# Norms of A's q and of C's q rank applied ahead of the scores, and softmax sums divided out of A's and C's outputs instead of their probabilities

## The chip, the cores and the metric

The kernel runs on one core of a Trainium2 chip. The metric is the device time of one execution in microseconds (us), as the median of several runs.

A core has five engines that run side by side and wait for each other through semaphores. PE (TensorE) multiplies matrices: it loads a stationary operand of up to 128x128 (shown as PEld) and streams the moving one past it, into a bank of PSUM. DVE (VectorE) does elementwise work and reductions, ACT (ScalarE) functions and copies, POOL (GpSimd) elementwise work at a lower rate, and SP (SyncE) issues the transfers (DMA) between memory and SBUF, the working memory. Each engine takes its own instructions in the order in which they were written to its queue.

## The reference

A bidirectional encoder of two layers on 512 tokens and 1024 channels, in float32. Each layer:

```python
h = rms_norm(x, ln1_g)
a_q, a_k, a_v, b_q, b_k, b_v, c_cq, c_ckv, c_kr, gates = split(h @ w_in)
# A: 8 heads of 64, 2 kv heads; q and k normed per head, then 2-D rotary
q = axial(rms_norm(a_q, q_g)) * 64 ** -0.5;  k = axial(rms_norm(a_k, k_g))
y_a = softmax(q k^T) v
# B: 8 heads with two maps of 32 each
p = softmax(q0 k0^T) - lam * softmax(q1 k1^T);  y_b = rms_norm(p v, sub_g) * (1 - lambda_init)
# C: latent attention; ranks 384 and 256, 8 heads of 64 + 32 rotary
q = rms_norm(c_cq, g) @ w_uq;  kv = rms_norm(c_ckv, g) @ w_ukv
y_c = softmax((q_nope k_nope^T + q_rope k_rope^T) * 96 ** -0.5) v
x = x + sum_n(sigmoid(gate_n) * (y_n @ w_branch_n)) @ w_out
x = x + relu(rms_norm(x, ln2_g) @ w_ff1) ** 2 @ w_ff2
```

and a last norm at the end.

## The kernel before

**Precision.** Products run in float32r, with each float32 operand split into a high part and a low rest. `hi` (ACT, L150) writes the high part, `lo` (DVE, L155, or L157 with a scale) the rest, `split` does both. A weight is fetched by SP, its high part `wh` is made by ACT (L60) and its rest `wl` by POOL or DVE (L63); in the attention stages all of these are POOL's. Each product is the sum of high x high, high x low and low x high, three matmuls.

**Order of the work.** `plan` lists items with a cost in us of products; `run` emits them in that order, fetching and splitting weights some us ahead. `defer(dt, f)` emits `f` once `dt` us of products have been emitted after the present point; `want` emits what is still due until a needed tile exists. `weave` spreads one list of items (gates, projections) between the items of another (attention). From the emitted program the order on each engine is then planned once, with estimated durations, before it runs; so an engine may have later work ahead of earlier work, but on the chip its order is fixed.

**Stages of a layer.** Projection of A's k and v, statistics of the stream, A's q (two halves of four heads, `a_q`), the start of B's q and k; A's attention, woven with the rest of B's projections; B's attention, woven with gates, A's branch products, C's ranks (`c_proj`), C's rotary (`c_rope`), values and first heads (`c_pair`); C's attention, woven with further gates and heads; the merge of the gated branches; the output product; the MLP.

**Attention.** `attend` has 32 units per mixer: a head and a tile of 128 queries. For each unit `probs` makes the scores (PE, two banks "S"), their maximum (DVE, L510) and the exponential with the sum over keys (ACT, L515). 5.5 us of products later the probabilities are turned (PE, four 128x128 transposes, L526) and split (L529 ACT, L530 DVE); 6.0 later they meet v (`pv`). After a head's four tiles `fix` adds two halves of the product (L539 ACT, L540 DVE); after a pair of heads `finish` makes the split output `y`, which the branch products read.

Where the change touches it:
- *A's q.* `post` of `a_q` makes the rotary of the raw q as two terms (`a_rope`: DVE, and half of the second term on POOL, L407) and adds them (L433). `late`, 14 us of products on, turns the rows (L263) and splits them (`a_G`), then calls `norm`: squares on POOL (L416), sums (L418), and the reciprocal roots `aR` (`rsqrt`, a dozen small DVE instructions, L169 to L180). `aR` isn't put on q: it multiplies the maximum (L514) and is the scale of the exponential.
- *C's q rank.* `rank` splits the raw rank straight out of PSUM, and late_q makes the factor `rq` from its sums of squares (L747, `rsqrt`, L755). `rq` scales the scores, as `aR` does. The kv rank is normed itself: diagonals of the factor (L302), a product that spreads it over the partitions, and a multiplication (L769).
- *Sums.* For A and C `normalise` takes the reciprocal of the sum (L519) and scales the 128x512 probabilities (L520).
- *B.* Its second map's weight is the reciprocal of its sum (L671) times minus lambda and the first map's sum (L672); L673 adds the second map's probabilities with this weight to the first's. B's output norm takes the first map's sum out again. Its `finish` spreads eight factors per pair to 128x512 (`bR`, L695), turns them on PE (`bT`, L702) and multiplies (L703).

Of the kernel before, what the change touches and what calls it, by code (L numbers as in the profile page):

```python
# [25 lines left out]
# pieces of 1024 columns per layer  # L26
# [11 lines left out]
# columns of the gain array  # L38
# [3 lines left out]
class Weight:  # L42
    """A piece of weights: loaded, then split into two float32r parts that add up to it."""
# [24 lines left out]
class Trunk:  # L68
# [24 lines left out]
    def run(self, plan):  # L93
        """Emits the items (cost, function, weights), the weights' loads and splits ahead of their use."""
# [29 lines left out]

# [41 lines left out]
    def rsqrt(self, dst, v, n):  # L166
# [5 lines left out]
        # a step of Newton's, then one of third order  # L172
# [30 lines left out]
    def tm_chunk(self, ws, per, width, xs, evac, post=None, late=None, lag=12.0, tags="LLLL"):  # L203
        """Items of a token-major product: one for each tile of 128 tokens, or, with weights in
        two pieces, one for each of these and each piece, two tiles to a bank."""
# [21 lines left out]
        def half(u, tt):  # L227
# [4 lines left out]
            for i, (l, r) in enumerate(p):  # L232
                # the bank's first product clears it for both tiles
# [25 lines left out]
    def transpose4(self, src, sl, name="tp"):  # L259
        """[tokens, 4, cols] of 128 columns to [128, 512 tokens] in a bank."""  # L260
# [6 lines left out]
    def stat_add(self, st, d, x):  # L267
        """Sums of squares over d = 0, 2, 4, 6 and over 1, 3, 5, and the squares of 7."""
# [15 lines left out]
    def col_sums(self, ps, xs, tts=range(4)):  # L284
        """Sums over the partitions of all of xs, a column for each 128 tokens, in one group."""
# [24 lines left out]
    def bcast_cols(self, col, name):  # L310
        """[128 tokens, 4] to [128, 512 tokens], the same row in each partition."""
# [31 lines left out]
    def layer_consts(self, l):  # L343
# [4 lines left out]
        # gains of A's q and k in the rotary tables  # L348
# [13 lines left out]
        # minus lambda of B  # L362
# [22 lines left out]
    def v_evac(self, vt, tt, ps, scale):  # L385
        """128 columns of two heads to [hi|lo] of the first and [lo|hi] of the second."""
# [5 lines left out]
    def a_rope(self, tq, nh, n):  # L392
        """Gain and axial rotary of each head's 64 columns, as the two terms of a sum."""
# [18 lines left out]
    def head_sumsq(self, e, x, sq, nh):  # L412
        """[128, 4 nh] sums of squares over each head's 64 columns."""
# [7 lines left out]
    def a_q(self, l, g):  # L421
        """The rows' norms of q stay out of it: they scale the scores."""
# [8 lines left out]
        def post():  # L431
            t1, t2 = self.a_rope(st["t"], 4, "q")
            nc.vector.tensor_tensor(t1, t1, t2, op=ALU.add)  # L433
            st["r"], st["f"] = t1, t2

        def norm():
            ss = self.head_sumsq(nc.gpsimd, st["t"], st["f"], 4)
# [3 lines left out]
            self.aR[g] = self.p.tile([128, 16], F32, tag="a_R", name="a_R", bufs=2)  # L441
            self.rsqrt(self.aR[g], ss, 16)

        def late():
# [8 lines left out]
            norm()  # L453
# [50 lines left out]
    def probs(self, mms, scale=None, z=None):  # L504
        """Scores of 128 queries: their exponentials and the sums of these."""
# [7 lines left out]
        if scale is not None:  # L513
            nc.vector.tensor_tensor(m, m, scale, op=ALU.mult)  # L514
        nc.scalar.activation(p, s, AF.Exp, bias=m, scale=1.0 if scale is None else scale, accum_out=z)  # L515
        return p, z

    def normalise(self, p, z):
        self.nc.vector.reciprocal(z, z)  # L519
        self.nc.vector.tensor_scalar(p, p, z, None, op0=ALU.mult)  # L520
# [21 lines left out]
    def attend(self, unit_probs, vt, finish, cost):  # L542
        """Items for the 8 heads' 4 tiles of queries; finish(pair, y) takes a pair's output."""
# [30 lines left out]
    def att_a(self):  # L574
        self.y = {}

        def probs(h, qt):
# [4 lines left out]
            i = qt * 4 + h % 4  # L582
            p, z = self.probs([(G[:, e, q], K[:, 0]), (G[r, e, q], K[r, 1])], self.aR[g][:, i : i + 1])
            self.normalise(p, z)
# [16 lines left out]
    def b_qk(self, l, n, hb):  # L601
        """q or k of four heads: rotary on the first 8 of each map's 32, then features on partitions."""
# [41 lines left out]
    def b_stack(self, h):  # L644
        """A head's two maps: q as [hi; lo; hi] and k as [hi; hi; lo] on 96 partitions."""
# [9 lines left out]
    def att_b(self, l):  # L655
        nc = self.nc

        def probs(h, qt):
            """The maps' difference times the first map's sum: the norm takes that out again."""
# [6 lines left out]
            if h % 2 == 0 and qt == 0:  # L666
                self.bz[h // 2] = self.p.tile([128, 8], F32, tag="bz", name="bz", bufs=2)
            i = 2 * qt + h % 2
            p0, z0 = self.probs([(Q[0:96, 0, q], K[0:96, 0])], z=self.bz[h // 2][:, i : i + 1])
            p1, z1 = self.probs([(Q[0:96, 1, q], K[0:96, 1])])  # L670
            nc.vector.reciprocal(z1, z1)  # L671
            nc.vector.scalar_tensor_tensor(z1, z1, self.nlam, z0, op0=ALU.mult, op1=ALU.mult)  # L672
# [12 lines left out]
        def sums(j, yt, sq):  # L685
# [4 lines left out]
            z = self.bz[j]  # L690
# [3 lines left out]
            R = self.tmp("bR", (128, 4, 2, 64))  # L694
            nc.vector.tensor_copy(R, rs.rearrange("p (t h) -> p t h", h=2).unsqueeze(3).to_broadcast([128, 4, 2, 64]))  # L695
            self.defer(3.0, lambda: scale(j, yt, R))

        def scale(j, yt, R):
            T = self.ps("T", "bT")
            Rf = R.rearrange("p t h f -> p t (h f)")  # L700
            for tt in range(4):
                nc.tensor.transpose(T[:, tt * 128 : (tt + 1) * 128], Rf[:, tt], self.ident)  # L702
            nc.vector.scalar_tensor_tensor(yt, yt, self.gsub, T, op0=ALU.mult, op1=ALU.mult)  # L703
# [7 lines left out]
    def c_proj(self, l):  # L711
        """The ranks' features on partitions; the norm of q's rank scales the scores."""
# [3 lines left out]
        def rank(n, j, gi, w):  # L716
            def f():
# [32 lines left out]
        def late_q():  # L750
            self.cf["q"] = st["q"]
            v = norm("q", 384)
            self.rq = self.p.tile([128, 4], F32, tag="c_rq", name="c_rq", bufs=1)
            self.rsqrt(self.rq, v, 4)
            nc.vector.tensor_scalar(self.rq, self.rq, C_SCALE, None, op0=ALU.mult)  # L755

        def late_kv():
            v = norm("kv", 256)
# [453 lines left out]
```

## Time and profile before

| | |
|---|---|
| median of 3 runs | 1964.0 us (1963.39 to 1965.02) |
| span of the profiled execution | 1961.6 us |
| share of the span: PE / PEld / DVE / ACT / POOL | 97% / 80% / 63% / 47% / 22% |

The profile is of one execution. Its span runs from the program's first to its last instruction; 1961.6 us of span stand against 1964.0 us of the median run. The page has parts: busy time of each engine; the chain of work that ended last; groups of instructions (source line, engine, operation, what is written and read, shapes, count, then busy time, mean duration of one, and the idle time of the engine in front of them with what ended it). Other views show the busy time by stretches of the span, the waits (engine and line that waited, for whom, us in total, times, longest), and single instructions in the order of time. Matmuls are pipelined: the time from one start to the next is what one costs PE, not its duration.

### The profile page before, as it was taken

Reading aid. Unit: us, or ns where it says so; the run is one execution under the profiler, and the core shown is the slowest. Engines: PE = TensorE matmul, PEld = TensorE weight load, DVE = VectorE, ACT = ScalarE, POOL = GpSimd, SP = SyncE. Lnnn points to the kernel's source line nnn. Section 1 sums busy time; section 2 is a strip of 40 time slices with the busy share of each in tenths; the row PEclk is TensorE's granted clock in tenths of the full one; section 3 lists DMA queues with packets and bytes.
Section 4 is the critical chain, followed back from the end, with each engine's and each line's share of the span. In section 5 each row is a group of like instructions: output and inputs, shape, how many; then the busy total and the mean of one; then the engine's idle time right before and its main releaser. Section 6 shows DMA issues by size and latency. Waiting matters only on the chain.

```text
span 1961.6 us, 26144 instructions
## 1 busy us (share of the span) xinstructions
PE 1893.2 (97%) x9848; PEld 1569.0 (80%) x9848; DVE 1227.5 (63%) x2232; ACT 916.9 (47%) x1658; POOL 427.1 (22%) x259
## 2 busy tenths in 40 slices
PE   8999989999999999999999999999999999999997
PEld 8888777777778888888898877777777788888886
DVE  7788888856665443444477889796565654334434
ACT  5466665754534331243245666556554334213332
POOL 4211232344235000000041112323431440000000
PEclk9999999999999999999999999999999999999998
DMA  4212322222123222223322033213230432223222
GB/s 156 67 41 69 109 79 68 80 80 91 45 93 122 97 97 97 97 97 113 113 92 65 28 96 103 83 44 96 79 93 33 137 99 91 97 95 102 98 96 68
DMA packets 63150, 171.83 MB, mean 88 GB/s; under 512 B 9520, under 2 KB 14000, under 8 KB 63024
## 3 DMA queue, kind: packets, MB, share of 16 engines
q1 hardware_dynamic: 63024, 170.16, 27.2%
q8 instruction: 78, 1.28, 0.3%
q14 instruction: 48, 0.39, 0.1%
HBM read 149.15 MB, written 4.19 MB: 78 GB/s over the span
## 4 chain that ended last, share of the span: by engine, by line
PE 78%; DVE 14%; ACT 3%; issue 2%; DMA 1%; SPq 1%; POOL 0%; DVEq 0%; POOLq 0%; ACTq 0%
PE ff L147 35%; PE gate L147 12%; PE sc L147 6%; PE br L147 5%; PE tm L234 5%; PE out L147 4%; PE pT L526 4%; PE pv L147 4%; PE c_rank L147 2%; DVE mg L919 1%; DVE mx L514 1%; DVE mx L510 1%; ACT p L515 1%; DVE p L673 1%; DVE wl L63 1%
## 5 line engine op out<-in xcount | busy, mean ns | idle before, releaser
L60 ACT CAST wh<-wr 128x1024 fp32r<-128x1024 f32 (+5 forms) x310 | 292.0, 942 | 645.8 <-PE ff L147 430.9
L63 POOL TENSOR_TENSOR wl<-wr,wh 128x1024 fp32r<-128x1024 f32 (+4 forms) x170 | 326.8, 1924 | 768.4 <-ACT wh L60 714.6
L63 DVE TENSOR_TENSOR wl<-wr,wh 128x1024 fp32r<-128x1024 f32 (+2 forms) x140 | 171.9, 1228 | 281.3 <-ACT wh L60 281.2
L147 PE MATMUL ff<-ff,wh 128*128 128x512 f32 (+1 forms) x1056 | 317.2, 383 | 0.0
L147 PE MATMUL ff<-xg,wh 128*128 128x512 f32 x1024 | 315.5, 389 | 0.0
L147 PE MATMUL gate<-xg,wh 128*128 128x512 f32 x768 | 243.5, 396 | 1.1 <-DVE c_K L155 1.1
L147 PEld LDWEIGHTS ff<-ff,wh 128*128 128x128 f32 x1056 | 196.3, 188 | 38.6
L147 PEld LDWEIGHTS ff<-xg,wh 128*128 128x128 f32 x1024 | 192.1, 188 | 39.6
L510 DVE TENSOR_REDUCE mx<-sc 128x1 f32<-128x512 f32 x256 | 174.0, 684 | 50.3 <-PE sc L147 49.6
L234 PE MATMUL tm<-wh,xg 128*128 128x256 f32 x1024 | 204.4, 291 | 0.0
L147 PE MATMUL ff<-ff,wl 128*128 128x512 f32 (+1 forms) x528 | 202.0, 383 | 0.0
L147 PE MATMUL ff<-xg,wl 128*128 128x512 f32 x512 | 199.4, 389 | 0.0
L147 PEld LDWEIGHTS gate<-xg,wh 128*128 128x128 f32 x768 | 141.4, 188 | 33.0 <-issue 4.4
L234 PEld LDWEIGHTS tm<-wh,xg 128*128 128x128 f32 x1024 | 165.8, 193 | 1.0 <-issue 0.5
L277 POOL TENSOR_TENSOR acc<-acc,sq 128x512 f32<-128x512 f32 x15 | 24.6, 1641 | 626.9 <-ACT sq L275 626.9
L529 ACT CAST pt<-pT 128x512 fp32r<-128x512 f32 x192 | 111.9, 584 | 84.3 <-PE pT L526 83.1
L530 DVE TENSOR_TENSOR pt<-pT,pt 128x512 fp32r<-128x512 f32 x192 | 131.4, 686 | 30.7 <-ACT pt L529 30.1
L147 PE MATMUL gate<-xg,wl 128*128 128x512 f32 x384 | 150.4, 392 | 0.0
L234 PE MATMUL tm<-wl,xg 128*128 128x256 f32 x512 | 145.8, 285 | 0.0
L526 PE MATMUL pT<-ident,p 128*128 128x128 f32 x768 | 120.5, 280 | 10.7 <-DVE p L673 8.6
L526 PEld LDWEIGHTS pT<-ident,p 128*128 128x128 f32 x768 | 87.6, 141 | 40.8 <-issue 26.2
L147 PEld LDWEIGHTS ff<-ff,wl 128*128 128x128 f32 x528 | 99.2, 188 | 19.5
(239 smaller groups left out, 3196.1 us busy)
## 6 DMA issues: line engine op xcount, KB each, us to landing
wr<-w SPq DMA_DIRECT2D x234, 512.0 KB, 3.5
wr<-w SPq DMA_DIRECT2D x52, 256.0 KB, 2.6
b_sq<-b_f SPq DMA_DIRECT2D x96, 64.0 KB, 2.4
b_sk<-b_f SPq DMA_DIRECT2D x96, 64.0 KB, 2.0
x<-xT SPq DMA_DIRECT2D x8, 256.0 KB, 5.6
c_Q<-c_qr SPq DMA_DIRECT2D x32, 64.0 KB, 2.4
c_K<-c_krf SPq DMA_DIRECT2D x16, 128.0 KB, 4.4
x<-xT SPq DMA_DIRECT2D x4, 512.0 KB, 6.0
```

The costliest lines, as they stand in the source:

```text
L60: t.nc.scalar.copy(wh, self.raw)
L63: e.tensor_tensor(wl, self.raw, wh.bitcast(F32), op=ALU.subtract)
L147: self.nc.tensor.matmul(out, l, r, start=(i == 0), stop=(i == n - 1))
L234: self.nc.tensor.matmul(ps, l, r, start=(u == 0 and i == 0 and tt % 2 == 0), stop=(u == 1 and tt % 2 == 1 and i == len(p) - 1))
L277: e.tensor_tensor(st[d % 2], st[d % 2], sq, op=ALU.add)
L510: nc.vector.tensor_reduce(m, s, axis=AX.X, op=ALU.max, negate=True)
L514: nc.vector.tensor_tensor(m, m, scale, op=ALU.mult)
L515: nc.scalar.activation(p, s, AF.Exp, bias=m, scale=1.0 if scale is None else scale, accum_out=z)
L526: nc.tensor.transpose(T[:, k], p[:, k * 128 : (k + 1) * 128], self.ident)
L529: nc.scalar.copy(h[:, :, q], T)
L530: nc.vector.tensor_tensor(lo[:, :, q], T, h[:, :, q].bitcast(F32), op=ALU.subtract)
L673: nc.vector.scalar_tensor_tensor(p0, p1, z1, p0, op0=ALU.mult, op1=ALU.add)
```

## The change

Four edits:
1. `a_q` squares the raw q on POOL at the start of `post`, ahead of the rotary. 3 us of products after `post`, `norm` makes the sums and reciprocal roots and multiplies the rotated rows, 128x1024, by them (DVE). `late` turns rows that are normed.
2. The q rank of C is treated as the kv rank: kept whole, and 9 + 2 us of products later multiplied by its spread factor and split.
3. Scores of A and C come out ready, so `probs` has no scale. Probabilities stay undivided. Each unit's sum goes to a column of a tile of eight per pair (`zcol`, three buffers, for B too); when a pair's output is there, `finish_plain` takes eight reciprocals, spreads them (`spread_pair`, B's code moved), and 2.5 us of products later turns them on PE, multiplies the output and splits it.
4. B's weight: `tensor_scalar` with two pointer scalars instead of `scalar_tensor_tensor`.

```diff
@@ a_q
         def post():
+            sq = self.s4("a_qs", (128, 4, 256), F32)
+            nc.gpsimd.tensor_tensor(sq, st["t"], st["t"], op=ALU.mult)
             t1, t2 = self.a_rope(st["t"], 4, "q")
             nc.vector.tensor_tensor(t1, t1, t2, op=ALU.add)
-            st["r"], st["f"] = t1, t2
+            st["r"], st["sq"] = t1, sq
+            self.defer(3.0, norm)
 
         def norm():
-            ss = self.head_sumsq(nc.gpsimd, st["t"], st["f"], 4)
+            ss, rs = self.small("ss", 16), self.small("a_R", 16)
+            nc.vector.tensor_reduce(ss, st["sq"].rearrange("p t (h f) -> p (t h) f", f=64), axis=AX.X, op=ALU.add)
...
-            self.aR[g] = self.p.tile([128, 16], F32, tag="a_R", name="a_R", bufs=2)
-            self.rsqrt(self.aR[g], ss, 16)
+            self.rsqrt(rs, ss, 16)
+            r = st["r"].rearrange("p t (h f) -> p (t h) f", f=64)
+            nc.vector.tensor_tensor(r, r, rs.unsqueeze(2).to_broadcast([128, 16, 64]), op=ALU.mult)
...
                 self.aG[2 * g + j] = G
-            norm()
@@ probs
-        if scale is not None:
-            nc.vector.tensor_tensor(m, m, scale, op=ALU.mult)
-        nc.scalar.activation(p, s, AF.Exp, bias=m, scale=1.0 if scale is None else scale, accum_out=z)
+        nc.scalar.activation(p, s, AF.Exp, bias=m, accum_out=z)
...
-    def normalise(self, p, z):
-        self.nc.vector.reciprocal(z, z)
-        self.nc.vector.tensor_scalar(p, p, z, None, op0=ALU.mult)
+    def zcol(self, h, qt):
+        if h % 2 == 0 and qt == 0:
+            self.zs[h // 2] = self.p.tile([128, 8], F32, tag="bz", name="bz", bufs=3)
+        i = 2 * qt + h % 2
+        return self.zs[h // 2][:, i : i + 1]
+
+    def spread_pair(self, rs):
+        R = self.tmp("bR", (128, 4, 2, 64))
+        self.nc.vector.tensor_copy(R, rs.rearrange("p (t h) -> p t h", h=2).unsqueeze(3).to_broadcast([128, 4, 2, 64]))
+
+        def turn():
+            T = self.ps("T", "bT")
+            Rf = R.rearrange("p t h f -> p t (h f)")
+            for tt in range(4):
+                self.nc.tensor.transpose(T[:, tt * 128 : (tt + 1) * 128], Rf[:, tt], self.ident)
+            return T
+
+        return turn
@@ finish_plain
         def f(j, yt):
+            rs = self.small("rz", 8)
+            self.nc.vector.reciprocal(rs, self.zs[j])
+            turn = self.spread_pair(rs)
+            self.defer(2.5, lambda: scale(j, yt, turn))
+
+        def scale(j, yt, turn):
+            self.nc.vector.tensor_tensor(yt, yt, turn(), op=ALU.mult)
             y = self.s4(f"y{n}")
             self.split(y, yt)
@@ att_b
-            nc.vector.scalar_tensor_tensor(z1, z1, self.nlam, z0, op0=ALU.mult, op1=ALU.mult)
+            nc.vector.tensor_scalar(z1, z1, self.nlam, z0, op0=ALU.mult, op1=ALU.mult)
@@ c_proj
-                if n == "q":
-                    x = self.s4("c_f")
-                    self.split(x, ps, g)
-                else:
-                    if j == 0:
-                        st["raw"] = self.s4("c_sq", dtype=F32)
-                    x = st["raw"][:, j]
-                    self.hi(x, ps, g)
+                if j % 2 == 0:
+                    st["raw"] = self.s4("c_sq", dtype=F32)
+                x = st["raw"][:, j % 2]
+                self.hi(x, ps, g)
...
         def late_q():
-            self.cf["q"] = st["q"]
-            v = norm("q", 384)
-            self.rq = self.p.tile([128, 4], F32, tag="c_rq", name="c_rq", bufs=1)
-            self.rsqrt(self.rq, v, 4)
-            nc.vector.tensor_scalar(self.rq, self.rq, C_SCALE, None, op0=ALU.mult)
+            dg = factor("q", 384, C_SCALE)
+            self.defer(2.0, lambda: spread("q", dg))
...
+        def spread(n, dg):
             ps = self.ps("T", "c_bc")
             self.spread(ps, dg)
             f = []
-            for x in st["kv"]:
+            for x in st[n]:
                 nc.vector.tensor_tensor(x, x, ps, op=ALU.mult)
                 f.append(self.s4("c_f"))
                 self.split(f[-1], x)
-            self.cf["kv"] = f
+            self.cf[n] = f
```

In A's and C's `probs` the scale argument and the call of `normalise` go.

More of the change, by code (lines that the diff above doesn't have):

```diff
@@ L574, in att_a @@
     def att_a(self):
-        self.y = {}
         def probs(h, qt):
@@ L693, in sums, with scale @@
             self.rsqrt(rs, v, 8)
[L694 to L703, printed above, removed]
+            turn = self.spread_pair(rs)
+            self.defer(3.0, lambda: scale(j, yt, turn))
+        def scale(j, yt, turn):
+            nc.vector.scalar_tensor_tensor(yt, yt, self.gsub, turn(), op0=ALU.mult, op1=ALU.mult)
             y = self.s4("yb")
@@ L750, in late_q, with factor @@
         def late_q():
[L751 to L764 removed]
+            dg = factor("q", 384, C_SCALE)
+            self.defer(2.0, lambda: spread("q", dg))
+        def late_kv():
+            dg = factor("kv", 256)
+            self.defer(2.0, lambda: spread("kv", dg))
+        def factor(n, width, scale=None):
+            r = self.small("c_r", 4)
+            self.rsqrt(r, norm(n, width), 4)
+            if scale is not None:
+                nc.vector.tensor_scalar(r, r, scale, None, op0=ALU.mult)
+            return self.diags(r)
+        def spread(n, dg):
             ps = self.ps("T", "c_bc")
@@ L935, in begin @@
         def begin():
-            self.aG, self.aK, self.aR, self.ys = {}, {}, {}, {"a": {}, "b": {}, "c": {}}
-            self.bz = {}
+            self.aG, self.aK, self.ys = {}, {}, {"a": {}, "b": {}, "c": {}}
+            self.zs = {}
             self.bf, self.bs, self.bV = {"q": {}, "k": {}}, {"q": {}, "k": {}}, {}
```

22 lines of the change are left out of this document (5 added, 17 removed).

## The prediction

> **What bounds the kernel now.** I read the page's busy times first, then busy time by stage, then what PE (TensorE) waits for, then single rows.
>
> ```profile
> span 1961.6 us, 26144 instructions
> PE 1893.2 (97%) x9848; PEld 1569.0 (80%) x9848; DVE 1227.5 (63%) x2232; ACT 916.9 (47%) x1658; POOL 427.1 (22%) x259
> ```
>
> PE is busy 97% of the span; only what is added to PE, or a wait of PE that goes or comes, can move the end. By stage of layer 0 (columns: stretch, its length, busy time and count of PE, PEld, DVE, ACT, POOL, granted clock, DMA share, GB/s):
>
> ```profile
> 55.00:71.00 16.00, 13.66 (x115) 13.45 (x113) 15.31 (x35) 6.63 (x11) 1.89 (x1) 0.99 0.25 91
> 75.00:187.00 112.00, 108.38 (x751) 91.23 (x750) 89.06 (x202) 69.81 (x146) 18.30 (x9) 0.98 0.16 48
> 187.00:369.00 182.00, 169.22 (x904) 139.66 (x903) 155.90 (x325) 113.48 (x247) 53.73 (x31) 0.98 0.29 84
> 369.00:577.00 208.00, 206.43 (x994) 160.49 (x993) 128.58 (x250) 109.04 (x203) 74.23 (x46) 1.00 0.24 75
> 577.00:590.00 13.00, 8.20 (x32) 5.65 (x31) 10.55 (x8) 3.77 (x5) 6.32 (x3) 0.86 0.56 195
> ```
>
> The rows are: end of the layer's first projections, A's attention, B's, C's, the merge behind C. In A's and C's attention PE has 3.6 and 1.6 us of idle time: the vector work taken out of these loops is work off the path. DVE (VectorE) is full at 55 to 71 (15.31 of 16) and nearly so in B. What PE waits for, both layers together:
>
> ```profile
> PE sc L147 <- ACT p L515: 10.4, 6, 2.7
> PE pT L526 <- DVE p L673: 8.6, 8, 2.1
> PE tp L263 <- DVE b_t L620: 4.7, 6, 1.5
> PE pv L147 <- DVE pt L530: 4.3, 4, 1.5
> PE tp L263 <- DVE a_G L155: 3.4, 2, 2.3
> ```
>
> The first, second and fourth, 23.3 us, are the attentions' vector chains, nearly all in B; this is what relief of DVE can win there at most.
>
> **What goes from DVE.** Groups (busy, mean ns of one):
>
> ```profile
> L514 DVE TENSOR_TENSOR mx<-mx,c_rq 128x1 f32<-128x1 f32 x64 | 30.0, 468 | 1.6
> L514 DVE TENSOR_TENSOR mx<-mx,a_R 128x1 f32<-128x1 f32 x64 | 20.5, 320 | 0.9
> L519 DVE RECIPROCAL z<-z 128x1 f32<-128x1 f32 x128 | 20.6, 161 | 24.0 <-ACT p L515 18.5
> L520 DVE TENSOR_SCALAR p<-p,z 128x512 f32<-128x512 f32 x128 | 62.8, 491 | 3.2
> L672 DVE SCALAR_TENSOR_TENSOR z<-z,nlam,bz 128x1 f32<-128x1 f32 x64 | 30.8, 481 | 1.1
> L671 DVE RECIPROCAL z<-z 128x1 f32<-128x1 f32 x64 | 10.2, 160 | 10.4 <-ACT p L515 9.6
> ```
>
> A and C lose 30.0 + 20.5 + 20.6 + 62.8 = 133.9 us of DVE time. In A's and C's loops this covers the new reciprocal, copy and product of each pair (at most L519's 0.16, and twice L520's 0.49 for a copy and a product of the same size: 1.1 a pair, 18 us for 16 pairs), so I cost those at nothing, except for the layer's last pair of C (below). If that cover were gone, A's stage (89 of 112 us busy) would still have room for the 4.6 us of its four pairs. The buffer that each pair's spread now takes costs nothing as long as A and C hold no more such tiles than B's stage does; bounded by the same rows of waits, since a late buffer would show as a wait for DVE.
>
> **What comes to PE.** Each of 16 pairs gets four transposes of the spread reciprocals, as B's pairs have now:
>
> ```profile
> 298.56 0.60 PE L702 MATMUL bT<-ident,bR 128*128 128x128 f32 x4
> 298.99 0.38 PE L526 MATMUL pT<-ident,p 128*128 128x128 f32 x2
> ```
>
> From start to start they hold PE for 0.43 us. 16 x 0.43 = 6.9; the two spreads of C's q factor, four products of the same size each, I take at the same price: 0.9. Sum **+7.8**, on a saturated engine; I see no cover in A and C. Bounds: 0.36 each without a change of operand between them (6.5) and 0.60, the group's busy time (10.8).
>
> **A's q norm ahead of the transposes.** Now the factor only has to be there at the first scores; then it has to be on the rows before PE turns them.
>
> ```profile
> 67.06 0.28 PE L234 MATMUL tm<-wh,xg 128*128 128x256 f32 x1
> 69.68 0.52 PE L263 MATMUL tp<-ident,b_t 128*128 128x128 f32 x3 [2.34 <-DVE a_G L155]
> 68.14 2.81 DVE L155 TENSOR_TENSOR a_G<-tp,a_G 64x512 fp32r<-64x512 f32 x4
> L433 DVE TENSOR_TENSOR a_t<-a_t,a_t 128x1024 f32<-128x1024 f32 x4 | 4.9, 1221 | 0.3
> L416 POOL TENSOR_TENSOR a_t<-a_tq 128x1024 f32<-128x1024 f32 x4 | 7.6, 1894 | 13.8 <-DVE a_t L433 13.8
> ```
>
> PE already stands 2.3 us at 69.68 for DVE. The new product over 128x1024 has two SBUF inputs like L433: 1.22 us, twice a layer, in front of the a_G parts for which PE waits, on a DVE that is 15.31 of 16 us busy: +2.4 a layer, **+4.9**. Lower bound 0 (the planner finds gaps earlier in the start). Upper: the square, 1.89 us, now stands on POOL in front of POOL's half of the rotary, which the DVE add waits for; with it 4.3 a layer, and a PE stall of that size brings slow clock, as here inside B:
>
> ```profile
> 279.15:282.40 3.25, 3.25 (x11) 2.67 (x10) 2.25 (x6) 2.35 (x5) 0.57 (x1) 0.50 0.00 0
> ```
>
> Half clock over 3.25 us loses 1.6: 5.9 a layer at most. The Trainium skill (TensorE: Matmul & The Clock Gate, Part 1) says that the array drops to half rate after an idle window of about 3.4 us and needs as long to come back; this row agrees with the half rate, at 0.50 over 3.25 us.
>
> **C's q rank scaled before its use.** The first product with the rank, and the factor, as they lie now, and the parts of the new chain:
>
> ```profile
> 344.56 0.28 PE L147 MATMUL tm<-wh,c_f 128*128 128x256 f32 x1
> 344.69 0.29 PE L147 MATMUL tm<-wl,c_f 128*128 128x256 f32 x1
> 347.65 0.16 DVE L755 TENSOR_SCALAR c_rq<-c_rq 128x4 f32<-128x4 f32 x1
> L302 DVE TENSOR_SCALAR dg<-ident,c_rkv 128x128 f32<-128x128 f32 x8 | 1.7, 278 | 0.0
> L769 DVE TENSOR_TENSOR c_sq<-c_sq,c_bc 128x512 f32<-128x512 f32 x4 | 2.7, 676 | 0.1
> L150 ACT ACTIVATE c_f<-c_sq 128x512 fp32r<-128x512 f32 x4 | 2.5, 632 | 0.0
> L155 DVE TENSOR_TENSOR c_f<-c_sq,c_f 128x512 fp32r<-128x512 f32 x4 | 2.7, 678 | 0.0
> ```
>
> The product starts at 344.56; the factor, which it doesn't need now, ends at 347.81. Behind that come four diagonals (1.11), the spread (0.43), a scaling (0.68) and a split (0.63 + 0.68): first part ready at 351.4, 6.8 us late. What PE can do instead: C's v products (24 x 0.12 by the first two rows = 2.9) and the first k products (6 x 0.23 = 1.4). Left over 2.5 a layer, **+5.0**. Lower bound 0, if B's last units fill the rest; upper 6.8 + 1.6 = 8.4 a layer, if the order on PE was planned with a rank ready sooner than it is. Queued behind: the rotary of q, its copies by SP into c_Q, and C's first scores; these I expect gates to cover.
>
> **Small ones.** C's last pair ends in the merge, where DVE is the busier engine (10.55 of 13 us): the product with the turned reciprocals there, 0.7 us a layer as L769, **+1.4** (0 to 2). PE's 4.7 us wait for L620 in A: half gone with the shorter queue, **-2.3** (0 to -4.7).
>
> **B's two pointer scalars.** A tensor_scalar with two pointers is not in the trace. L672 takes 481 ns (as slow as now, gain 0), L671 next to it 160; I take 160, the nearer in kind, since it too reads one tensor: DVE gets back 30.8 - 10.2 = 20.6 us. What L672 waited for:
>
> ```profile
> 204.87 3.62 POOL L63 TENSOR_TENSOR wl<-wr,wh 128x1024 fp32r<-128x1024 f32 x2 [10.38 <-ACT wh L60]
> 205.99 1.28 DVE L672 SCALAR_TENSOR_TENSOR z<-z,nlam,bz 128x1 f32<-128x1 f32 x1
> 207.20 0.68 DVE L905 TENSOR_TENSOR gz<-gate,rbc 128x512 f32<-128x512 f32 x1
> 219.17 1.64 DVE L672 SCALAR_TENSOR_TENSOR z<-z,nlam,bz 128x1 f32<-128x1 f32 x1
> 220.84 0.75 DVE L673 SCALAR_TENSOR_TENSOR p<-p,z 128x512 f32<-128x512 f32 x1
> ```
>
> The first of them stands while POOL works. At 219.17 the next instruction is L673, which reads two tensors from SBUF as well: the wait passes to it, and all but 0.2 of 1.64 stays. At 205.99 the next one, L905, reads PSUM and could run meanwhile: 0.68 of 1.28 is won. Between these I take a third of 20.6, 6.9 us of DVE, and half of that where PE waits: **-3.4** (0 to -20.6). The Trainium skill (SBUF — State Buffer, Who interferes with whom) says that a DVE instruction with two SBUF inputs is blocked by a POOL instruction that reads SBUF, and one with a single input, outside the two-port modes, is not. The long rows agree for L672; by that rule the edit frees L672 wholly, and the sum by it alone would be rival 2's; but it also leaves L673 blocked.
>
> **Sum.** 7.8 + 4.9 + 5.0 + 1.4 - 2.3 - 3.4 = +13.4 on the profiled 1961.6, so 1975.0; the median of the runs, 1964.0, lies 2.4 above that execution: **1977**.
>
> **Rivals.** (1) *Only PE's own work shows*: planner and slack absorb both late chains. For it: within B, PE takes up later products where an operand is missing. Against: PE's order is fixed before the run, and stands 2.3 us at 69.68 already. 7.8 + 1.4 - 5.7 = +3.5: 1967. (2) *Faster*: the port wait does not pass on, and all 20.6 us of L672 come off PE's 23.3 us of waits, C's rank being in time with DVE so relieved. 7.8 + 4.9 + 1.4 - 2.3 - 20.6 = -8.8: 1955. It decides from about 16 of the 20.6 on; against it speaks the row at 220.84. (3) *Both chains late in full*: 7.8 + 11.8 + 16.8 + 1.4 - 5.7 = +32.1: 1996. For it: DVE saturated at both places, and the slow clock behind a stall; against: 4.3 us of other PE work by C's rank.
>
> **How the numbers follow.** Forecast 0.45 (its own range 1970 to 1985), rival 1 0.20, rival 2 0.15, rival 3 0.20. The range reaches to rivals 2 and 3: 1955 to 1997. Within 0.2% is 3.9 us, about what a measurement of this kernel can tell from no change: rival 1 is the same; forecast and rival 3, 0.65, are slower; rival 2, 0.15, faster.
>
> **What would show it.** PE: 72 more products of 128x128, about 0.43 us a group. A wait of PE for transposes of a_t where there is none now, or a longer one for a_G. PE's first product with C's q rank at 349 or later, with a wait for c_f, and a rank factor that ends no earlier than 347. L672's row near 0.16 us, L673's mean above the present 779 ns. I am wrong if PE's waits for p and L673 shrink by more than 10 us, if c_f comes without a wait, or if A's stage shrinks by more than it gains in transposes.

## The result and the profile after

The changed kernel takes **1979.8 us** (median of 4 runs, 1978.9 to 1980.8) beside 1963.7 us for the kernel before on the same chip: ratio 1.0087, 95% interval 1.0073 to 1.0102. It is slower. The forecast was 1977 with a range of 1955 to 1997. The number held, but by errors that cancelled, as the stretches show.

The first row of the page of the changed kernel, then busy time by stretch of layer 0, first for the kernel before and then for the changed one. The six stretches are cut at the same products of PE in both: from the first statistics to A's first scores, to B's first scores, to the first product of C's ranks, to C's first heads; then, from C's first scores 7.2 us later in both, C's attention, and the merge. Columns: stretch, its length, busy time and count of PE, PEld, DVE, ACT and POOL, granted clock, DMA share, GB/s.

```profile
span 1977.1 us, 25992 instructions
PE 1899.1 (96%) x9928; PEld 1576.3 (80%) x9928; DVE 1140.5 (58%) x1914; ACT 904.7 (46%) x1664; POOL 428.0 (22%) x259
```

```profile
22.50:78.60 56.10, 52.53 (x426) 51.97 (x425) 46.93 (x109) 25.21 (x52) 21.67 (x20) 0.97 0.28 95
78.60:189.30 110.70, 107.08 (x731) 89.51 (x730) 90.92 (x205) 70.49 (x147) 20.42 (x9) 0.98 0.15 45
189.30:283.00 93.70, 86.58 (x444) 70.69 (x443) 81.95 (x148) 56.91 (x121) 26.30 (x14) 0.98 0.35 103
283.00:359.90 76.90, 71.65 (x412) 60.39 (x410) 64.70 (x160) 46.38 (x105) 23.11 (x14) 0.98 0.20 56
367.10:555.90 188.80, 187.23 (x906) 144.89 (x906) 114.36 (x233) 102.46 (x192) 66.79 (x40) 1.00 0.24 73
555.90:578.80 22.90, 22.90 (x106) 18.66 (x105) 17.18 (x20) 8.45 (x14) 9.46 (x7) 1.00 0.28 93
```

```profile
22.70:83.60 60.90, 52.59 (x425) 51.82 (x425) 52.47 (x111) 25.09 (x52) 21.22 (x20) 0.97 0.26 85
83.60:195.10 111.50, 108.27 (x743) 91.22 (x742) 71.40 (x119) 67.23 (x147) 20.48 (x9) 0.98 0.15 47
195.10:282.10 87.00, 84.93 (x448) 70.13 (x447) 74.93 (x148) 55.18 (x120) 25.16 (x13) 1.00 0.38 110
282.10:362.60 80.50, 71.44 (x420) 60.19 (x418) 69.69 (x169) 48.37 (x110) 24.69 (x14) 1.00 0.19 53
369.90:563.70 193.80, 189.74 (x918) 146.99 (x918) 86.74 (x147) 99.29 (x192) 66.58 (x40) 0.99 0.23 71
563.70:587.20 23.50, 23.50 (x110) 19.03 (x109) 18.02 (x22) 8.38 (x14) 9.71 (x7) 1.00 0.31 91
```

DVE's relief in A (90.92 to 71.40 us) and C (114.36 to 86.74) is there and bought neither stage any time. B's row, the third, is the surprise: 6.7 us shorter. The start, the fourth row and C are 4.8, 3.6 and 5.0 us longer. The same stretches of layer 1 were cut in the same way. Beside the growth of both layers together stands the prediction's sum, dealt out to the places that its terms name (16 turned groups, four transposes each: 8 for A, 6 in C, 2 in the merge; on the chip the turn of A's last pair stands behind B's first scores, so A's row holds 3 a layer and B's 1):

| stretch | predicted | layer 0 | layer 1 | both |
|---|---|---|---|---|
| start, to A's first scores | +4.9 | +4.8 | +3.9 | +8.7 |
| A's attention | +1.1 | +0.8 | +0.8 | +1.6 |
| B, to the ranks' first product | -3.4 | -6.7 | -6.8 | -13.5 |
| the ranks' products | 0 | -0.5 | -0.5 | -1.0 |
| ranks' last product to C's first heads | +5.9 | +4.2 | +4.3 | +8.5 |
| C's attention | +2.6 | +5.0 | +4.6 | +9.6 |
| merge | +2.3 | +0.6 | +0.5 | +1.1 |

The rows sum to +15.0; the span grew by 15.5. Each stretch is read from one execution, and one stretch of 3.4 us at half clock more or less moves it by 1.7. So +13.4 was met by two errors of opposite sign: some 10 us too little gain in B, and some 12 too little loss around it. That the sum came out is luck.

What PE waits for in the changed kernel, both layers (us in total, times, the longest; some waits that changed little are left out):

```profile
PE tp L263 <- DVE a_t L446: 6.6, 2, 5.4
PE tp L263 <- DVE a_kr L491: 5.1, 2, 2.7
PE pT L544 <- DVE p L692: 5.0, 6, 1.2
PE tp L263 <- DVE b_t L642: 4.6, 6, 1.4
PE c_bc L147 <- DVE dg L302: 4.3, 2, 2.1
PE pT L544 <- DVE rsy L171: 4.0, 2, 2.0
PE tm L147 <- DVE c_K L155: 3.2, 2, 1.6
PE pT L544 <- DVE yt L615: 2.9, 2, 1.5
PE sc L147 <- ACT p L516: 2.8, 4, 1.1
PE tm L147 <- ACT c_f L150: 2.4, 2, 1.2
```

New are the waits for A's normed rows (L446), for the diagonals and first part of C's rank (L302, L150), and for the product with the turned reciprocals (L615). Longer are those for the rotated rows of A's k (a_kr: 2.2 before) and for the low parts of the heads' keys (c_K: 0.4 before). The exponentials' wait fell from 10.4 to 2.8 us and the one for B's mixed probabilities from 8.6 to 5.0; between the ranks' products a wait of 2.0 us a layer behind a small instruction of a root (L171) is new, so PE's stalls there did not shrink.

Three places, row by row (start, duration, what was done, idle time before). First the start, with the square that now stands ahead on POOL and A's norm, then C's rank, then a pair's turn in C:

```profile
39.38 1.89 POOL L432 TENSOR_TENSOR a_qs<-a_tq 128x1024 f32<-128x1024 f32 x1
39.61 2.75 DVE L491 TENSOR_TENSOR a_kr<-a_t,a_t 128x1024 f32<-128x1024 f32 x1
...
51.45 1.89 POOL L432 TENSOR_TENSOR a_qs<-a_tq 128x1024 f32<-128x1024 f32 x1 [5.51 <-ACT a_tq L428]
51.53 1.84 DVE L174 TENSOR_TENSOR rst<-rst,rsh 128x16 f32<-128x16 f32 x1
54.96 2.34 POOL L63 TENSOR_TENSOR wl<-wr,wh 128x1024 fp32r<-128x1024 f32 x1
55.07 2.26 DVE L179 TENSOR_TENSOR rst<-rst,rsh 128x16 f32<-128x16 f32 x1
57.57 1.22 DVE L446 TENSOR_TENSOR a_t<-a_t,a_R 128x1024 f32<-128x1024 f32 x1
58.94 1.94 PE L263 MATMUL tp<-ident,a_t 128*128 128x128 f32 x8 [5.38 <-DVE a_t L446]
...
346.50 1.13 PE L147 MATMUL c_bc<-dg,ones 128*128 128x128 f32 x8 [2.14 <-DVE dg L302]
349.58 0.38 PE L147 MATMUL tm<-wh,c_f 128*128 128x256 f32 x1 [1.21 <-ACT c_f L150]
...
494.33 0.63 PE L535 MATMUL bT<-ident,bR 128*128 128x128 f32 x4 [0.42 <-DVE bR L529]
496.40 0.69 DVE L914 TENSOR_TENSOR gc<-gate,rbc 128x512 f32<-128x512 f32 x1
497.01 0.68 DVE L615 TENSOR_TENSOR yt<-yt,bT 128x512 f32<-128x512 f32 x1
497.74 0.66 PE L544 MATMUL pT<-ident,p 128*128 128x128 f32 x4 [1.47 <-DVE yt L615]
```

In A, PE stands 5.38 us, and only 1.22 of that is the product. Two of the dozen small instructions that make the roots take 1.84 and 2.26 us, where the same ones elsewhere take 0.17 us; each stands for as long as a POOL instruction of 1.89 or 2.34 us. Earlier, at 39.61, the sum of A's rotated k meets the new square and takes 2.75 us, where it took 1.31 before; PE waits 2.7 us for it instead of 1.2. In layer 1 the second cause is the larger one: a weight's split ahead of that sum meets the square there (2.94 us, 1.50 before), PE waits 2.4 us for k instead of 1.0, runs soon after for 3.4 us at a granted clock of 0.50, and waits only 1.3 us for the normed rows. In C, the turned reciprocals lie in one of the two T banks. DVE comes to their product 2.1 us after the turn has ended, behind L914 among others, and the next probabilities' transposes, which need that bank, wait.

### The profile page after: what moved, and what is told of

The parts are those of the page before. It is cut to its first block, busy times and chain, and to the rows that moved or that the text cites. A ratio compares the mean times of both kernels' runs of the same rounds, so it can differ in the third digit from the quotient of the medians.

```text
span 1977.1 us, 25992 instructions
## 1 busy us (share of the span) xinstructions
PE 1899.1 (96%) x9928; PEld 1576.3 (80%) x9928; DVE 1140.5 (58%) x1914; ACT 904.7 (46%) x1664; POOL 428.0 (22%) x259
## 4 chain that ended last, share of the span: by engine, by line
PE 83%; DVE 10%; ACT 3%; issue 2%; DMA 1%; SPq 1%; POOL 0%; DVEq 0%; POOLq 0%; ACTq 0%
PE ff L147 35%; PE gate L147 13%; PE sc L147 6%; PE tm L234 6%; PE br L147 5%; PE pT L544 4%; PE out L147 4%; PE pv L147 4%; PE c_rank L147 2%; DVE mg L928 1%; PE tm L147 1%; DVE b_t L642 1%; PE tp L263 1%; DVE p L692 1%; PE tm L247 1%
## 5 line engine op out<-in xcount | busy, mean ns | idle before, releaser
L516 ACT ACTIVATE p<-sc,mx 128x512 f32<-128x512 f32 x256 | 176.3, 691 | 84.5 <-DVE mx L513 78.0
```

The costliest lines, as they stand in the source:

```text
L516: nc.scalar.activation(p, s, AF.Exp, bias=m, accum_out=z)
```

## The experiments

The runs of the kernel before on the same chip, medians 1961.4, 1962.9 and 1963.8 us in the three sets, stand beside each set; ratios are to them.

### The two pointer scalars: undone, and alone

```diff
-            nc.vector.tensor_scalar(z1, z1, self.nlam, z0, op0=ALU.mult, op1=ALU.mult)
+            nc.vector.scalar_tensor_tensor(z1, z1, self.nlam, z0, op0=ALU.mult, op1=ALU.mult)
```

> The changed kernel with edit 4 undone: B's weight is a scalar_tensor_tensor again, all else is as changed. My theory: the wait behind POOL that this instruction had only moved to the next one, which adds the second map's probabilities; undoing the edit moves it back. The two groups together stay at 80 to 82 us of DVE time (80.8 with the edit), and the time stays within 3 us of the changed kernel's 1979.8. Rival: the edit is what made B 13.5 us shorter over both layers; then the time is about 1993, and the exponentials' wait in B is back (10.4 us before the change, 2.8 behind it).

The second kernel is the one before, with that line changed the other way.

> The kernel before with edit 4 alone. My theory: the wait passes to the next instruction; the two groups stay at about 81 us together, and the time within 3 us of 1963.7. Rival: the edit itself frees B; then about 1950, with B 6.7 us shorter in each layer.

Undone in the changed kernel: 1986.1 us, 1.0122 (1.0107 to 1.0137). Alone: 1963.7 us, 1.0008 (0.9998 to 1.0018). Groups (busy, mean ns of one) of the changed kernel, of the one with the edit undone, and of the edit alone:

```profile
L692 DVE SCALAR_TENSOR_TENSOR p<-p,z 128x512 f32<-128x512 f32 x64 | 63.7, 995 | 1.0
L691 DVE TENSOR_SCALAR z<-z,nlam,bz 128x1 f32<-128x1 f32 x64 | 17.2, 269 | 0.7
```

```profile
L692 DVE SCALAR_TENSOR_TENSOR p<-p,z 128x512 f32<-128x512 f32 x64 | 49.7, 776 | 1.1
L691 DVE SCALAR_TENSOR_TENSOR z<-z,nlam,bz 128x1 f32<-128x1 f32 x64 | 24.5, 382 | 0.9
```

```profile
L673 DVE SCALAR_TENSOR_TENSOR p<-p,z 128x512 f32<-128x512 f32 x64 | 56.4, 882 | 1.1
L672 DVE TENSOR_SCALAR z<-z,nlam,bz 128x1 f32<-128x1 f32 x64 | 17.2, 269 | 0.9
```

The wait does pass on: the new form costs 269 ns (258 to 275, all 64), the old form 216 on the mean in the kernel before without POOL's splits (below), and the next one's mean rises from 779 to 882 ns in the kernel before and from 776 to 995 in the changed one. Of the 20.6 us that rival 2 gave to the edit, nothing reaches the end in the kernel before. But the two groups together are not the 80 to 82 us that I expected everywhere: 80.7 before and 80.9 with the change, 74.2 and 73.6 in these two. And undoing the edit in the changed kernel costs about 7 us (1.0122 against 1.0087), spread over B (+1.0 in each layer), the ranks (+1.1, +2.0), the stretch behind them (+0.7, +1.4) and C of layer 0 (+1.4), less 1.5 each in the start and A of layer 0. So the first expectation fails, and of the second only the time holds. The Trainium skill (SBUF — State Buffer, Who interferes with whom) says that a DVE instruction with two SBUF inputs contends with a POOL instruction that reads SBUF, and that one with at most one, outside the two-port modes, does not; the rows agree, 269 ns on the mean of all 64 of the new form, and 995 for the two-input one behind it.

### A's norm back on the scores

Edit 1 undone (`a_q` as before; the factor scales the maxima and the exponentials):

```diff
-            self.defer(3.0, norm)
...
-            nc.vector.tensor_tensor(r, r, rs.unsqueeze(2).to_broadcast([128, 16, 64]), op=ALU.mult)
...
+            nc.vector.tensor_tensor(m, m, scale, op=ALU.mult)
+        nc.scalar.activation(p, s, AF.Exp, bias=m, scale=1.0 if scale is None else scale, accum_out=z)
```

> The changed kernel with edit 1 undone: A's scores are scaled by the norm of q again, as before, while A's outputs are still divided by the sums. My theory: the norm ahead of the transposes is the whole of the start's growth (5.0 and 3.9 us in the two layers), as PE there waits 5.4 us for the product by the norm; without it the start is as long as before, about 1971. The scaling of the maxima comes back to DVE in A, where DVE has room, and costs under 1 us. Rival: the start is late for DVE anyhow, or the maxima's scaling (64 instructions of about 320 ns) costs A's attention what the start wins; then 1977 to 1980.

1976.8 us, 1.0073 (1.0056 to 1.0089). The start is as long as before in both layers (0.0, 0.0), so edit 1, the square moved ahead included, is its whole growth, as expected. But only 2.1 us of 8.7 come back in the span (1977.1 to 1975.0): A is 0.8 and 0.7 us longer than with the change, B's first stretch 1.1 in each layer, the ranks 1.7 and 1.6. These come to 7.0 us where under 1 was expected, and the 1971 us fall with that. The time is at the edge of the rival's 1977 to 1980, but only 1.5 us of the loss lie in A, where the maxima's scaling is; why B and the ranks lose too was not tested.

### C's norm back on the scores

Edit 2 undone (`c_proj` as before, the factor again the scale in `probs`):

```diff
-            dg = factor("q", 384, C_SCALE)
-            self.defer(2.0, lambda: spread("q", dg))
...
+            self.rsqrt(self.rq, v, 4)
+            nc.vector.tensor_scalar(self.rq, self.rq, C_SCALE, None, op0=ALU.mult)
```

> The changed kernel with edit 2 undone: the norm of C's q rank scales C's scores again, while C's outputs are still divided. My theory: the factor, spread, product and split ahead of the rank's first use are the 4.2 us that each layer grew between the rank's products and the first heads; without them about 1971, and PE has no wait for the rank's parts there. Rival 1: the rank's late split is also what makes B shorter (its split work leaves the place where B's second half needs DVE); then B grows back by some us and the time stays at 1976 to 1980. Rival 2: the growth there is the planner's, not the chain's: the place stays 4 us longer.

1973.3 us, 1.0054 (1.0037 to 1.0072). From the ranks' last product to the first heads 31.5 us, as long as before (31.7): the chain is the growth, and rival 2 falls. The stretch of the ranks' own products, where the raw rank is split again, is 3.6 and 2.4 us longer than with the change. Of 8.5 us, 6.7 remain in the span (1977.1 to 1970.4): between the theory and rival 1.

### Edits 3 and 4 alone, and edit 3 in A alone

The first leaves out edits 1 and 2. The second then divides C's probabilities again:

```diff
-            p, _ = self.probs(..., self.zcol(h, qt), self.rq[:, qt : qt + 1])
+            p, z = self.probs(..., None, self.rq[:, qt : qt + 1])
+            self.normalise(p, z)
```

> Edits 1 and 2 undone together: the norms of A's q and C's q rank scale the scores again, edits 3 and 4 stay. If the two edits' costs add up (their runs alone: 0.14% and 0.33% off the change's 0.87%), this is 1.0040 of the kernel before, with the starts as long as before, the stretch from C's rank to C's first heads 4.3 us shorter a layer than with the change, B's first stretch (first scores to the rank's first product) still 6 us shorter a layer than before, and C's attention still 5 us longer. Rival: undoing edit 1 cost 1 to 2 us in each of A's and B's stretches, undoing edit 2 cost 2 to 3 us between the rank's products, because the maxima's scaling is back on DVE; with both back those losses add, and B's gain is gone: 1.006 or more.

> As the run with edits 3 and 4 only, but C's probabilities are divided again, and C's outputs not: edit 3 in A alone, with edit 4. It tells where B's gain and C's loss come from. Theory: C's attention grows because each pair's turned reciprocals hold one of the two T banks that the probabilities' transposes use, so it is back at 188.8 us a layer (5 less); B's first stretch is shorter because A's division is gone from DVE, so it stays at 86 to 88 us (before: 93.7). Then 0.995 to 0.998 of the kernel before. Rival: B's gain comes from the plan as a whole and not from A's division; then B is back at 93.7 and the time 1.002 or more.

Edits 3 and 4: 1971.4 us, 1.0047 (1.0032 to 1.0062), against 1.0040 if the two costs add: they do, within the interval. With edit 3 in A alone: 1961.7 us, 0.9992 (0.9983 to 1.0001), no change. So dividing **C's** outputs costs 0.55%, or 10.8 us: C is back at 188.8 us in both layers, from 193.7 and 194.7. B's first stretch stays at 88.2 and 88.4 us: its gain comes with A's outputs, and is used up for the most part by A (+1.6, +3.1) and the ranks (+1.8, +2.0). The expected 0.995 to 0.998 was too good, and the rival's B of 93.7 us did not come either.

### The turn in another bank

```diff
-            T = self.ps("T", "bT")
+            T = self.ps(tag, "bT")
...
-            turn = self.spread_pair(rs)
+            turn = self.spread_pair(rs, "L")
```

Only A's and C's pairs use the L bank; the second kernel has the same on top of edits 3 and 4 alone.

> The changed kernel, with A's and C's reciprocals turned in one of the three L banks in place of one of the two T banks (B's as before). Theory: the changed kernel's wait of the probabilities' transposes for the product with the turned reciprocals (2.9 us over two places, 1.5 the longest) and the half-clock stretch behind it in C go: C's attention 3 us a layer shorter (about 190.5), in all about 6 us less, 1.0057 of the kernel before. Rival 1: the L banks are as short, gates and heads wait for them instead; C stays at 193.5 or grows. Rival 2: C's growth is DVE's order of work and not the bank; C stays at 193.5 and the wait for the product stays.

> Edits 3 and 4 alone, with A's and C's reciprocals turned in L banks: the two changes of the other runs together. If they add, 1.0040 less 0.0030: 1.001 of the kernel before. Rival: the plan moves B again, and the sum is missed by 3 us or more either way.

C does as the theory says: the wait for L615 is gone and so is the slow clock behind it. As PE's order at the seam of C and the merge differs in this kernel, the two are taken together: 214.3 and 213.8 us, against 217.3 and 216.9 with the change and 211.7 before. The bank is worth 3.1 us a layer, and of C's and the merge's growth 2.6 and 2.1 us are left, which is four turned groups at the 0.59 us that the runs without splits give (below). The kernels are slower all the same: 1990.9 us, 1.0143 (1.0126 to 1.0160), and 1988.7, 1.0134 (1.0119 to 1.0149). B's first stretch, whose own code is untouched, went from 87.0 to 96.4 us, and in the second kernel from 88.2 to 102.4. The second kernel's rival foresaw that the plan moves B; the first one's rivals did not. In PE's order the turn of A's last pair stands at another place of B's beginning, and in the first kernel 6.8 us of B's first stretch run at half clock in each layer, none with the change.

### B without POOL's splits

So B's length was what had to be explained. The trace of before has the pattern (first fence, the cause of a stall of PE of 2.7 us), and the changed kernel's same place (second fence; PE's stall there is 1.1 us):

```profile
250.10 4.23 POOL L63 TENSOR_TENSOR wl<-wr,wh 128x512 fp32r<-128x512 f32 x2 [7.53 <-ACT wh L60]
250.67 1.26 DVE L176 TENSOR_TENSOR rst<-rsy 128x8 f32<-128x8 f32 x1
251.96 2.39 DVE L177 TENSOR_TENSOR rst<-rst,rsh 128x8 f32<-128x8 f32 x1
255.66 0.69 ACT L515 ACTIVATE p<-sc,mx 128x512 f32<-128x512 f32 x1 [3.78 <-DVE mx L510]
```

```profile
254.04 1.28 POOL L63 TENSOR_TENSOR wl<-wr,wh 128x512 fp32r<-128x512 f32 x1 [4.84 <-ACT wh L60]
254.00 1.88 DVE L692 SCALAR_TENSOR_TENSOR p<-p,z 128x512 f32<-128x512 f32 x1
255.79 0.15 DVE L176 TENSOR_TENSOR rst<-rsy 128x8 f32<-128x8 f32 x1
255.98 0.17 DVE L177 TENSOR_TENSOR rst<-rst,rsh 128x8 f32<-128x8 f32 x1
```

Before, two splits on POOL hold two tiny instructions of B's output norm for 3.3 us more than their 0.16, the maxima queue behind them, and ACT and PE behind those. With the change one shorter split meets one instruction. In the experiment the weights' low parts are left out in the attention stages of both kernels; the high part stands in for them. Both kernels' order of work is planned anew without the splits.

```diff
+            if t.POOLW == 5:
+                self.parts = wh, wh
+                return self.parts
```

> The kernel before, with the weights' low parts left out in the attention stages (the high part stands in for them, so the sums have as many products as before): POOL makes no splits there, and nothing else of that size stands in DVE's way. It leaves out part of the computation. Theory: B's first stretch of 93.7 us is about 84 us of products and some 9.6 us of stalls and slow clock that come from DVE instructions standing behind POOL's splits; so without splits 84 to 87 us. Rival: the stalls come from DVE's own work and order; 91 us or more.

> The changed kernel, with the weights' low parts left out in the attention stages in the same way. Theory: the change made B's first stretch 6.7 us shorter only because the splits fell elsewhere; without splits it is within 1.5 us of the kernel before's without splits (84 to 87 us), and the change then costs more than its 15.5 us of span: about 15.5 + 2 x 6 = 27 us. Rival: B's gain is real relief of DVE (the division of A's probabilities, the port waits of the weight instruction); then B stays 4 us or more shorter than in the kernel before without splits.

B's first stretch in layer 0, kernel before and changed kernel:

```profile
188.90:273.70 84.80, 84.43 (x438) 69.02 (x437) 70.11 (x151) 56.64 (x123) 0.00 (x0) 1.00 0.40 113
```

```profile
195.30:280.10 84.80, 84.69 (x445) 69.46 (x443) 71.45 (x152) 56.60 (x125) 0.00 (x0) 1.00 0.39 112
```

Equal, with PE busy throughout (layer 1: 84.5 and 84.7). B's 93.7 us before were 84.8 of products and 8.9 of meetings with POOL and the slow clock behind them; the change met POOL less, and that is its gain. The first table agrees: B's stretch holds 148 DVE instructions in both kernels, and they were busy for 81.95 us before and 74.93 with the change. The rival, a relief of DVE that works without POOL, falls: it would have left 4 us between the two. Whether the meetings grew fewer by the order alone, or also because A's division no longer stood on DVE at B's beginning, these runs don't tell apart: without stalls no relief could show. Without the splits the change costs 27.1 us of span (1915.6 to 1942.7; medians 1914.0 and 1943.2), as expected: the meetings of the kernel before had hidden nearly half of the price. If anything 27 is low, as the profiled execution of the kernel before without splits has in layer 1's C a stretch of 10.2 us at half clock, behind a wait for an exponential, that layer 0 does not have; why is open.

The two kernels also price a turned group. In A's stretch PE is busy throughout in both, and it grew from 104.4 to 106.2 us by three groups: 0.59 us each.

### Shorter splits on POOL

If a DVE instruction waits out the POOL instruction that it meets, POOL's should be short. Edit 3 in A with edit 4, and the kernel before, each with:

```diff
-            e.tensor_tensor(wl, self.raw, wh.bitcast(F32), op=ALU.subtract)
+            n = 512 if e is t.nc.gpsimd else self.cols
+            for o in range(0, self.cols, n):
+                s = slice(o, min(o + n, self.cols))
+                e.tensor_tensor(wl[:, s], self.raw[:, s], wh[:, s].bitcast(F32), op=ALU.subtract)
```

> The run with edit 3 in A alone and edit 4, with each of POOL's weight splits made in pieces of 512 columns, so that no one of them stands longer than 1.3 us (2.4 before). Theory: a DVE instruction with two inputs in SBUF waits out the POOL instruction that it meets; with pieces half as long the longest waits fall from 2.4 to 1.3 us, PE's stalls in B with them, and the stretches of B shrink by 2 to 4 us a layer: 0.995 to 0.998 of the kernel before. Rival: the waits add up over the pieces (a chain of small instructions meets each piece in turn), and the fixed cost of twice as many pieces makes POOL later: 0.999 or more.

> The kernel before with POOL's weight splits in pieces of 512 columns. The same theory and rival on the other order of work: 0.995 to 0.998 of the kernel before, or 0.999 and more.

**1940.5 us, 0.9877 (0.9861 to 0.9893)**, and **1941.1 us, 0.9889 (0.9872 to 0.9906)**: both beat both kernels, by more than twice the most that was expected. POOL's splits in the kernel before, in that kernel with halves, and C's scaling of maxima in the same two (count, busy, mean ns):

```profile
L63 POOL TENSOR_TENSOR wl<-wr,wh 128x1024 fp32r<-128x1024 f32 (+4 forms) x170 | 326.8, 1924 | 768.4 <-ACT wh L60 714.6 <-PE tp L263 11.9 <-PE pT L526 11.9
...
L514 DVE TENSOR_TENSOR mx<-mx,c_rq 128x1 f32<-128x1 f32 x64 | 30.0, 468 | 1.6
```

```profile
L66 POOL TENSOR_TENSOR wl<-wr,wh 128x512 fp32r<-128x512 f32 (+1 forms) x272 | 354.8, 1321 | 727.0 <-ACT wh L60 678.9 <-PE pT L529 23.8 <-DMA b_sk<-b_f 9.9
...
L517 DVE TENSOR_TENSOR mx<-mx,c_rq 128x1 f32<-128x1 f32 x64 | 17.1, 268 | 1.6
```

POOL works 28.0 us longer, and still the tiny instruction's mean falls from 468 to 268 ns, and DVE's busy time, on 2232 instructions in both, from 1227.5 to 1192.5 us. The waits do not add up over the pieces as the rival had it. The gain is wider than B, where I had looked for it: of the kernel before's 17.4 us of span, A gives 4.2 and 2.7, B's first stretch 2.9 and 2.5, and the stretch of the output product 1.1 and 2.9. The two versions' intervals overlap, so A's edit adds nothing measurable to it. The order of work was planned anew here too; how much of the gain is shorter waits and how much other meetings was not separated.

## Why the prediction was right, and where not

The direction was right for a sound reason: PE gets more products, and two chains now stand in front of it. The size came out by luck. B's gain was missed by 10 us, and the losses around it by 12, and these two have nothing to do with each other in the prediction.

**PE's added products (+7.8): right in kind, too small.** PE has 80 more products, not 72: a spread is eight in the trace, not four, and holds PE for 0.89 us from start to start (346.50 to 347.39). A turned group costs 0.59 us by A's stretch without splits, close to the upper bound of 0.60 and not the 0.43 that was taken. Together that would be an estimate of 11.2 us: 16 x 0.59 and 2 x 0.89. The sentence that the pair's new buffer costs nothing looked at the tile in SBUF; the buffer that counted is the T bank in PSUM. By the runs it is 3.1 us a layer in C and the merge. So C and the merge, whose eight groups and products on DVE were put at 4.9 us, came to 10.7: eight groups at 0.59 and twice 3.1 make 10.9.

**A's norm (+4.9): place right, too small for the start.** I charged the product of 1.22 us, kept the square for the upper bound, and left the dozen small instructions of the roots out of the chain, though they move ahead of PE's transposes with it. Two of them meet POOL for 3.8 us in layer 0. The square costs too, but elsewhere than the bound had it: DVE meets it in front of k's transposes, in both layers. The start grew by 8.7 us, and all of it goes when the edit is undone; but the whole kernel then wins 2.1, as A, B and the ranks grow.

**C's rank (+5.0, with the spreads 5.9): right in place and kind, under by 2.6.** PE's first product with the rank starts at 349.58 with a wait for it, as foretold; the diagonals came late as well (2.14 us), which I had not counted as a wait of its own.

**A's wait for L620 (-2.3): did not come.** 4.7 us before, 4.6 after. So A's row, +1.6 against +1.1, is near by two errors as well. **The merge (+2.3): +1.1**, which is its two turned groups at 0.59; the product there cost nothing that shows.

**B (-3.4): wrong.** The argument that the wait passes on to the next instruction holds; the 3.4 us that the edit was to win did not come, as alone it is worth nothing in the kernel before (1.0008). The new form takes 269 ns, not 160. And I said that I would be wrong if PE's waits for p and L673's shrank by more than 10 us, and they shrank by 11.2 (10.4 + 8.6 to 2.8 + 5.0). The failed step is the tacit one that B changes only where its code does. Its work met POOL's splits less, and that gave the 13.5 us, as the equal stretches without splits show; with edit 3 in A and edit 4 alone 10.9 of them are there. Which single shift in the order does it was not found; the other bank shows that a shift as small as a turn's place can take it back.

**The rivals.** Rival 1, both chains absorbed, fell at the start and at the rank. Of rival 2's gain 13.5 of 20.6 us came, but from another cause. Rival 3's two full delays, 11.8 and 16.8 us, came out at 8.7 and 8.5. The forecast was right as a sum; of the table's rows only the start, A's attention and the rank's were within a factor of two.

## What to carry to other kernels

Where one engine's instructions wait out another's, as DVE's did POOL's here, a queue's length depends on which instructions happen to meet; a change anywhere ahead of it moves the meetings, and gains or losses of about a per cent appear in code that was not touched (B's first stretch: 87.0 to 102.4 us). Before crediting an edit, take the meetings away in both versions and compare. And keep the instructions that others wait out short: two of 512 columns for one of 1024 cost POOL 28 us, and the kernel came out 1.1% faster.

When a reduction's factor moves from behind a product to ahead of it, charge the whole chain that makes it, small instructions included, and every PSUM bank that it holds until the last reader is done.

## What the runs showed of the hardware

The clock fell to half without a long stop of PE. In C of the changed kernel (stretches, columns as above):

```profile
494.00:498.60 4.60, 2.80 (x14) 1.68 (x14) 3.69 (x7) 4.40 (x8) 1.82 (x1) 1.00 0.27 102
498.70:502.10 3.40, 3.40 (x8) 2.42 (x9) 2.20 (x4) 1.83 (x5) 0.45 (x1) 0.51 0.46 154
```

PE was busy for 2.80 of 4.60 us, its longest wait there 1.47 us, and then ran 3.4 us at a granted clock of 0.51, worth 1.7 us. The prediction's citation of the Trainium skill (TensorE: Matmul & The Clock Gate, Part 1) had an idle window of about 3.4 us as the condition; that length agrees with how long the slow stretch lasts, not with how long PE must stand, which was less than half of it. With the turn in the other bank the wait and the slow stretch were gone from C in both layers.

A tensor_scalar with two pointer scalars on 128x1 takes 269 ns, against 160 for the reciprocal beside it and 216 for the scalar_tensor_tensor that it replaces (means; the last in the kernel before without POOL's splits): where POOL holds nothing up the edit is a loss of 53 ns.
